# Tokens as the stationary side of the second MLP product in three of four groups, with the sums turned back by DVE and DMA

## The chip, the cores and the metric

One Trainium2 chip; the kernel runs on one of its cores. The metric is the time of one execution on the device in microseconds (us). The kernel before takes 1535.57 us, the median of 3 runs (1535.53 to 1535.76).

The engines are named as in the profile: PE is TensorE (matmul), PEld its loading of the stationary operand, DVE is VectorE, ACT ScalarE, POOL GpSimd, SP SyncE. In a matmul one operand stands still in the array (stationary, 128x128) and the other streams through (moving, up to 512 columns); the product has the stationary side's columns as its partitions and the moving side's columns as its row. Sums gather in PSUM, in banks of 512 columns.

## The reference

A decoder layer on 256 tokens (and 16 meta tokens) of width 2048: a token mixer, then a squared-ReLU MLP with 8192 inner columns, then a norm. The change touches the MLP alone:

```
def squared_relu_mlp(xn, w1, w2):
    return jnp.square(jax.nn.relu(xn @ w1)) @ w2
...
h = h + squared_relu_mlp(rmsnorm(h, norm_mlp_g[l]), w_ff1[l], w_ff2[l])
return rmsnorm(h, final_norm_g)[:, N_META:]
```

All in float32.

## The kernel before

**Layout.** The residual stream lies transposed in SBUF: `ht` is 128 partitions x 16 tiles x 256 tokens, where tile j holds model columns 128j to 128j+127 on the partitions. All operands are split in two parts for the multiplication, `hi` (rounded to the matmul's type) and `lo` (the rest), and a product is hi·hi + hi·lo + lo·hi.

**The MLP** runs over NG = 4 groups of 2048 inner columns (second half of `trunk`, the loop over `g`). In each group:

- *first product*, 16 steps f: `gemm2(next_weights(), x2)` makes one tile of 128 inner columns x 256 tokens; `relu2` squares it and splits it into `a[:, f, 0, :]` (hi) and `a[:, f, 1, :]` (lo);
- *second product*, 16 steps j: `gemm2(next_weights(), a)` makes one tile of 128 model columns x 256 tokens out of the group's 2048 inner columns, and `add_residual` adds it to `ht[:, j, :]`: one ACT copy of the second half of the bank and two DVE adds.

In the last group the last NL = 4 tiles are made apart, in two token halves, so that the final norm and the stores can start early; this part stays as it is.

**One `gemm2`** goes over k = 0 to 15 with two matmuls each (`mac2`). In both, the weights are the stationary side and tokens move: the weights' hi against 512 columns (the tokens' hi and lo, 256 each), and the weights' lo against 256 (the tokens' hi).

```
nc.tensor.matmul(steps(ps), hi, steps(row(x)), start=first, stop=False)
nc.tensor.matmul(steps(ps[:, 0:NT]), lo, steps(x[:, 0, :]), start=False, stop=last)
```

`steps` is an access that reads and writes the columns in runs of four elements, 16 apart, in four passes.

**The weights** lie in HBM as 128x2048 chunks in the order of use, `w_all`; a chunk of the second product has 16 k x 128 output columns. `next_weights` brings one in as two pieces (`weight_half`): SP issues one DMA of 512 KB (128 partitions x 4 KB) into a `raw` buffer, ACT casts it to `hi` (L126), DVE subtracts to `lo` (L127). There are five `raw` buffers and five of `w` (hi and lo). A `raw` buffer is free after DVE's subtraction, a `w` buffer after PE's last matmul on it.

**The order** on each engine is made by a scheduler ahead of time from the order of the code and a timeline of its own; each engine then works through its queue strictly in that order. Thus ACT's casts stand some pieces ahead of the copies that wait for PE. `later(n, fn)` holds a function back until n further products have been issued.

**Pools.** PSUM has the pools `pg` (3 banks) and `px` (5). In SBUF, `gat` holds the MLP's small tiles; its tag `o` (8 KB a partition, 2 buffers) serves the output at the end. `keep` with tag `s1` holds `a`.

Of the kernel before, what the change touches and what calls it, by code (L numbers as in the profile page):

```python
# [7 lines left out]
F32 = mybir.dt.float32  # L8
# [3 lines left out]
AF = mybir.ActivationFunctionType  # L12
ALU = mybir.AluOpType
# [3 lines left out]
P = 128  # L17
D = 2048
KT = D // P
# [9 lines left out]
NG = 4  # L29
MASKED = -1e30  # L30
BIG = 3.0e38
RAW = 5
NL = 4
# [32 lines left out]
def trunk(ctx: ExitStack, tc: tile.TileContext, hT, w_small, w_all, consts, w_alpha2, out):  # L66
    nc = tc.nc
    serial = [0]

    def nm(s):  # L70
        serial[0] += 1
        return f"{s}_{serial[0]}"

    const = ctx.enter_context(tc.tile_pool(name="const", bufs=1))
    keep = ctx.enter_context(tc.tile_pool(name="keep", bufs=1))
    wp = ctx.enter_context(tc.tile_pool(name="wp", bufs=5))
# [3 lines left out]
    px = ctx.enter_context(tc.tile_pool(name="px", bufs=5, space=PSUM))  # L80
# [3 lines left out]
    def bank(pool, s):  # L84
        return pool.tile([P, 512], F32, tag="bank", name=nm(s))
# [4 lines left out]
    def later(n, fn):  # L90
        waiting.append([n, fn])

    def issued():
        for e in list(waiting):
            e[0] -= 1
            if e[0] <= 0:
                waiting.remove(e)
                e[1]()
# [6 lines left out]
    chunk = [0]  # L105
    HK = KT // 2

    def pair(meta=False):
        n = HK * P
        w = wp.tile([P, 2 * n + 64], F32R, tag="w", name=nm("w"))  # L110
        a, b = (0, 20) if meta else (24, 24)
        return [w[:, at : at + n].rearrange("p (k m) -> p k m", m=P) for at in (a, n + b)]
# [18 lines left out]
    def next_weights(keep_hi=None, meta=False):  # L131
        c = chunk[0]
        chunk[0] += 1
        parts = []
        for i in range(2):
            hi, lo, step = weight_half(c, i, None if keep_hi is None else keep_hi[:, HK * i : HK * (i + 1), :], meta)
            step(0, HK)
            parts.append((hi, lo))
        return lambda k: (parts[k // HK][0][:, k % HK, :], parts[k // HK][1][:, k % HK, :])

    def steps(ap):

        return ap.rearrange("p (i a e) -> p a i e", a=4, e=4)
# [93 lines left out]
    def operand(pool, name, nk=KT, at=0, **kw):  # L237

        t = pool.tile([P, at + nk * 2 * NT], F32R, name=nm(name), **kw)
        return t[:, at:].rearrange("p (k o t) -> p k o t", o=2, t=NT)  # L240
# [18 lines left out]
    def take(*shape):  # L259
        n = 1  # L260
        for d in shape:
            n *= d
        ap = room[:, at_room[0] : at_room[0] + n]
        at_room[0] += n
        if len(shape) == 2:
            ap = ap.rearrange("p (a b) -> p a b", b=shape[1])
        return ap
# [4 lines left out]
    def gain(i, k):  # L272
        return h[:, k, NA + i : NA + i + 1]
# [8 lines left out]
    acc = take(4, NA)  # L282
# [50 lines left out]
    for s in range(KT // 2):  # L333
        if s + 3 < KT // 2:
            with tc.issue_after(load_stage(s + 3, 0).ins):
                load_h(nc.sync, 2 * s + 6, 2)
            last = load_stage(s + 3, 1).ins
        wa, wb = stages[s]
        for kk in range(2):
            k = 2 * s + kk  # L340
# [15 lines left out]
        at = [(w[0][:, c], w[1][:, c]) for w, n in ((wa, 4), (wb, 3)) for c in range(n)]  # L356
# [35 lines left out]
    for i in range(2):  # L392
        w = pair(meta=True)[0]
# [17 lines left out]
    both = take(NA)  # L411
# [252 lines left out]
    ps = bank(pg, "psa")  # L664
    for k in range(KT):
        if k == HK:
            norm1()
        w = small[k // HK][:, k % HK, :]
# [171 lines left out]
    for j0 in range(0, KT, 2):  # L840
        gates = ahead if j0 == 0 else [gate() for _ in range(4)]
        w = next_weights()
        for j in range(2):
            t = total(gemm2(w, of, k0=8 * j, nk=8))
            nc.vector.tensor_tensor(gates[2 * j], gates[2 * j], t, op=ALU.mult)
        for j in range(2):
            t = total(gemm2(next_weights(), og))
# [7 lines left out]
    gat = ctx.enter_context(tc.tile_pool(name="gat", bufs=2, reuse_waits="tile"))  # L855
# [3 lines left out]
    ht = h[:, :, NM:NA]  # L859
    x2 = operand(keep, "x2", at=56, tag="s2")  # L860

    def square_sum(j, acc):
        if j == 0:
            nc.scalar.activation(acc, ht[:, j, :], AF.Square)
        else:
            sq = gat.tile([P, NT], F32, tag="hsq", name=nm("hsq"))
            nc.scalar.activation(sq, ht[:, j, :], AF.Square)  # L867
            nc.gpsimd.tensor_tensor(acc, acc, sq, op=ALU.add)  # L868
# [22 lines left out]
    def relu2(a, f, ps):  # L891
# [3 lines left out]
        nc.vector.tensor_tensor(s, t, t, op=ALU.mult)  # L895
        split_to(a[:, f, 0, :], a[:, f, 1, :], s)

    acc = gat.tile([P, NT], F32, tag="acc", name="acc3", bufs=1)
    for g in range(NG):
        a = operand(keep, "a", at=16, tag="s1")  # L900
        held = []
        for f in range(KT):
            ps = gemm2(next_weights(), x2, pool=px if g == 0 and f < 3 else pg)
            if g == 0 and f == 0:
                held.append(ps)
                continue
            if g == 0 and f == 1:
                relu2(a, 0, held.pop())
            relu2(a, f, ps)
        last = g == NG - 1  # L910
        for j in range(KT - NL if last else KT):
            add_residual(j, gemm2(next_weights(), a))
            if last:
                square_sum(j, acc)
                nc.scalar.activation(ht[:, j, :], ht[:, j, :], AF.Identity, scale=gain(2, j))
                if j == 0:
                    tc.keep_in_program_order(nc.scalar.preload_act_table_set("natural_log_exp_and_others"))


    whi = keep.tile([P, 8 + NL * KT * P + 56], F32R, tag="s2", name="whi_last")[:, 8 : 8 + NL * KT * P].rearrange(  # L920
# [2 lines left out]
    for n in range(NL):  # L923
        j, ps = KT - NL + n, bank(pg if n < 3 else px, "ps")
        w = next_weights(whi[:, n])
# [148 lines left out]
```

## Time and profile before

| what | value |
|---|---|
| median of 3 runs | 1535.57 us (1535.53 to 1535.76) |
| the profiled execution, its own time | 1535.16 us |
| its span, first to last instruction | 1533.5 us |
| mean granted clock of TensorE | 0.998 |
| second product of the first group | from 925.17 us of the span |
| second product of the third group | from 1266.50 to 1351.84 us |
| `hi` cast on ACT (L126), 128x1024 | 1048 ns |
| `lo` subtraction on DVE (L127), 128x1024 | 1225 ns |
| DMA of one weight piece, issue to landing | 4.5 us median |

Times in the views count from the first instruction. A row of the timeline gives the start, the length, the engine, the line, output<-inputs and how many instructions were merged; a PE length is modelled and overlaps the next, so the distance between two starts is what a matmul costs. A row of the windows gives the length of the window, then busy us and number of instructions of PE, PEld, DVE, ACT and POOL, then the granted clock, the DMA engines' busy share and GB/s. A row of a group gives busy us and mean ns, then the idle time ahead and who ended it.

### The profile page before, as it was taken

What the parts mean: (1) busy time and instruction counts of PE and PEld (TensorE: products, weight loads), DVE (VectorE), ACT (ScalarE), POOL (GpSimd) and SP (SyncE); (2) the same over time, 40 slices, a digit from 0 to 9 for tenths busy, and PEclk for the clock granted to TensorE, in tenths of its full rate; (3) what the DMA queues carried; (4) which work ended last, traced back from release to release, by engine and by line L of the source; (5) the groups of instructions that cost most, each with busy time, mean ns of one, the idle gap of its engine ahead of it and who ended that gap; (6) DMA issues with size and microseconds to landing.
All of it is one profiled execution on the core that took longest, in us unless ns stands there. A gap on an engine that the chain in (4) does not pass through costs nothing.

```text
span 1533.5 us, 25353 instructions
## 1 busy us (share of the span) xinstructions
PE 1522.3 (99%) x9812; PEld 1399.9 (91%) x9812; DVE 1072.2 (70%) x1659; ACT 794.4 (52%) x1271; POOL 130.2 (8%) x213
## 2 busy tenths in 40 slices
PE   9999999999999999999999999999999999999997
PEld 8999999999999999999999999999999999999997
DVE  7898858586666666666787876667766776667665
ACT  7766444555555544544666544445444454444563
POOL 6012010111100000000011000000000000000012
PEclk9999999999999999999999999999999999999999
DMA  9545555565555565655565566655565556555562
GB/s 320 172 153 176 182 162 188 160 212 170 166 167 188 197 198 197 195 199 199 188 209 195 197 198 197 200 195 195 195 203 197 198 196 199 197 197 200 194 195 96
DMA packets 86600, 293.08 MB, mean 191 GB/s; under 512 B 9112, under 2 KB 16800, under 8 KB 86352
## 3 DMA queue, kind: packets, MB, share of 16 engines
q1 hardware_dynamic: 85872, 289.62, 57.4%
q8 instruction: 77, 1.26, 0.3%
q0 software_dynamic: 176, 1.12, 0.2%
q10 hardware_dynamic: 432, 0.72, 0.1%
q14 instruction: 43, 0.35, 0.1%
HBM read 289.32 MB, written 2.11 MB: 190 GB/s over the span
## 4 chain that ended last, share of the span: by engine, by line
PE 96%; DVE 2%; ACT 1%; issue 1%; DMA 0%; POOL 0%; SPq 0%; POOLq 0%; DVEq 0%; ACTq 0%
PE ps L149 50%; PE ps L150 26%; PE psa L154 5%; PE psa L158 4%; PE psa L156 4%; PE ps L364 1%; PE ps L943 1%; PE ps L366 1%; DVE w L127 1%; PE ps L927 0%; DMA raw<-w_all_dram 0%; PE pa L562 0%; PE po L620 0%; DVE room L434 0%; POOL o L991 0%
## 5 line engine op out<-in xcount | busy, mean ns | idle before, releaser
L127 DVE TENSOR_TENSOR w<-raw,w 128x1024 fp32r<-128x1024 f32 x522 | 644.8, 1235 | 260.5 <-ACT w L126 251.3
L126 ACT CAST w<-raw 128x1024 fp32r<-128x1024 f32 x522 | 547.1, 1048 | 275.2 <-PE ps L150 210.1
L149 PE MATMUL ps<-x,w 128*128 128x512 f32 x1952 | 654.7, 381 | 0.0
L150 PE MATMUL ps<-x,w 128*128 128x256 f32 x1952 | 535.7, 274 | 0.0
L149 PEld LDWEIGHTS ps<-x,w 128*128 128x128 f32 x1952 | 366.5, 188 | 62.4
L150 PEld LDWEIGHTS ps<-x,w 128*128 128x128 f32 x1952 | 366.7, 188 | 0.0
L149 PE MATMUL ps<-a,w 128*128 128x512 f32 x960 | 320.2, 380 | 0.0
L150 PE MATMUL ps<-a,w 128*128 128x256 f32 x960 | 263.3, 274 | 0.0
L149 PEld LDWEIGHTS ps<-a,w 128*128 128x128 f32 x960 | 180.3, 188 | 30.9
L154 PE MATMUL psa<-x,w 128*128 128x272 f32 x640 | 181.9, 285 | 0.0
L150 PEld LDWEIGHTS ps<-a,w 128*128 128x128 f32 x960 | 180.3, 188 | 0.0
L158 PE MATMUL psa<-x,w 128*128 128x272 f32 x640 | 179.8, 282 | 0.0
L156 PE MATMUL psa<-x,w 128*128 128x272 f32 x624 | 176.1, 282 | 0.0
L187 ACT COPY evb<-ps 128x256 f32<-128x256 f32 x160 | 59.4, 371 | 205.1 <-PE ps L150 203.5
L190 DVE TENSOR_TENSOR evt<-ps,evb 128x256 f32<-128x256 f32 x158 | 67.0, 424 | 80.1 <-ACT evb L187 79.7
L154 PEld LDWEIGHTS psa<-x,w 128*128 128x128 f32 x640 | 120.2, 188 | 0.2
L158 PEld LDWEIGHTS psa<-x,w 128*128 128x128 f32 x640 | 120.2, 188 | 0.1
L156 PEld LDWEIGHTS psa<-x,w 128*128 128x128 f32 x624 | 117.6, 188 | 0.0
L868 POOL TENSOR_TENSOR acc<-acc,hsq 128x256 f32<-128x256 f32 x26 | 26.5, 1017 | 737.6 <-ACT hsq L867 737.6
L149 PE MATMUL ps<-og,w 128*128 128x512 f32 x256 | 85.8, 380 | 0.0
L149 PE MATMUL ps<-y,w 128*128 128x512 f32 x256 | 85.4, 380 | 0.0
L872 ACT COPY evb<-ps 128x256 f32<-128x256 f32 x76 | 28.2, 371 | 103.3 <-PE ps L150 102.3
(297 smaller groups left out, 1471.2 us busy)
## 6 DMA issues: line engine op xcount, KB each, us to landing
raw<-w_all_dram SPq DMA_DIRECT2D x537, 512.0 KB, 4.5
raw<-w_all_dram SPq DMA_DIRECT2D x8, 384.0 KB, 6.7
h<-hT_dram SPq DMA_DIRECT2D x8, 275.0 KB, 6.8
negc<-fdram POOLq DMA_DIRECT2D x1, 1088.0 KB, 7.9
out_dram<-o SPq DMA_DIRECT2D x2, 512.0 KB, 2.6
raw<-w_all_dram SPq DMA_DIRECT2D x2, 256.0 KB, 3.7
room<-w_small_dram SPq DMA_DIRECT2D x1, 320.0 KB, 8.1
out_dram<-o ACTq DMA_DIRECT2D x1, 320.0 KB, 3.1
```

The source lines that it names most:

```text
L126: nc.scalar.copy(hi[:, k, :], r)
L127: nc.vector.tensor_tensor(lo[:, k, :], r, hi[:, k, :].bitcast(F32), op=ALU.subtract)
L149: nc.tensor.matmul(steps(ps), hi, steps(row(x)), start=first, stop=False)
L150: nc.tensor.matmul(steps(ps[:, 0:NT]), lo, steps(x[:, 0, :]), start=False, stop=last)
L154: nc.tensor.matmul(steps(ps[:, X_LO]), hi, steps(x_lo[:, k]), start=first, stop=False, skip_group_check=True)
L156: nc.tensor.matmul(steps(ps[:, 0:NA]), lo, steps(x_hi[:, k]), start=False, stop=last and hi is None, skip_group_check=True)
L158: nc.tensor.matmul(steps(ps[:, 0:NA]), hi, steps(x_hi[:, k]), start=False, stop=last, skip_group_check=True)
L187: nc.scalar.copy(b, ps[:, NT:512])
L190: nc.vector.tensor_tensor(t, ps[:, 0:NT], b, op=ALU.add)
L364: nc.tensor.matmul(steps(ps), hi, steps(row(x[:, k])), start=st, stop=False)
L868: nc.gpsimd.tensor_tensor(acc, acc, sq, op=ALU.add)
L872: nc.scalar.copy(b, ps[:, NT:512])
```

## The change

In groups 0 to 2 the second product has its sides exchanged. Its 2048 output columns are taken in four blocks b of 512. For each k, 128 tokens of `a` are the stationary side and 512 weight columns the moving one; two token halves t give two banks, `pt`. The six matmuls of a k are, for each t: a-hi with w-hi, a-hi with w-lo, a-lo with w-hi. The result has tokens on the partitions. It is gathered over the groups in a new tile `rows` (2 halves x 2048 columns; 16 KB a partition): copied by ACT in group 0, added by DVE in 1 and 2.

The weights of a block come from four chunks at once (`wide_weights`): each of its eight pieces has two k and four chunks' 128 columns, 512 KB as before in runs of 1 KB, and ACT and DVE write hi and lo so that the 512 columns of a k lie in a row.

In group 2, `turn_back(b)` brings a block back to the layout of `ht`: two DVE transposes of 32x32 squares, 16 DMAs from POOL's queue that move the squares between partition groups within one tile of tag `o` (32 partitions x 8 runs x 32 elements each, 32 KB), and four adds on POOL into `ht`. The last group's second product is as before.

```
+    def wide_weights(q):
+
+        c0, k0 = chunk[0], 4 * q
+        parts = []
+        for i in range(2):
+            raw = wp.tile([P, HK * P], F32, tag="raw", name=nm("raw"), bufs=RAW)
+            hi, lo = (t.rearrange("p k m -> p (k m)").rearrange("p (k c m) -> p k c m", k=2, m=P) for t in pair())
+            r = raw.rearrange("p (c k m) -> p c k m", k=2, m=P)
+            cols = slice((k0 + 2 * i) * P, (k0 + 2 * i + 2) * P)
+            nc.sync.dma_start(r, w_all[c0 : c0 + 4, :, cols].rearrange("c p (k m) -> p c k m", m=P))
+            r = r.rearrange("p c k m -> p k c m")
+            nc.scalar.copy(hi, r)
+            nc.vector.tensor_tensor(lo, r, hi.bitcast(F32), op=ALU.subtract)
+            parts.append([t.rearrange("p k c m -> p k (c m)") for t in (hi, lo)])
+        if q == 3:
+            chunk[0] += 4
+        return lambda k: tuple(t[:, k % 2, :] for t in parts[k % 4 // 2])
...
+    rows = gat.tile([P, 2, D], F32, name="rows", bufs=1)
+
+    def turn_back(b):
+
+        both = gat.tile([P, KT * P], F32, tag="o", name=nm("turn"))
+        tr = both[:, 0:1024].rearrange("p (t f) -> p t f", t=2)
+        for t in range(2):
+            nc.vector.transpose(tr[:, t, :], rows[:, t, 512 * b : 512 * b + 512])
+        back = both[:, 1024:]
+        for c in range(4):
+            for i in range(4):
+                src = both[32 * c : 32 * c + 32, 0:1024].rearrange("p (e i r) -> p e i r", i=4, r=32)[:, :, i, :]
+                dst = back[32 * i : 32 * i + 32].rearrange("p (e c r) -> p e c r", c=4, r=32)[:, :, c, :]
+                nc.gpsimd.dma_start(dst, src)
+        for j in range(4):
+            r = ht[:, 4 * b + j, :].rearrange("p (t r) -> p t r", t=2)
+            nc.gpsimd.tensor_tensor(r, r, back.rearrange("p (t j r) -> p t j r", t=2, j=4)[:, :, j, :], op=ALU.add)
+
+    def token_rows(g, b, a):
+
+        pt = [bank(px, "pt") for _ in range(2)]
+        for k in range(KT):
+            if k % 4 == 0:
+                w = wide_weights(k // 4)
+            hi, lo = w(k)
+            for t, ps in enumerate(pt):
+                ah, al = (a[:, k, o, P * t : P * t + P] for o in range(2))
+                nc.tensor.matmul(steps(ps), ah, steps(hi), start=(k == 0), stop=False)
+                nc.tensor.matmul(steps(ps), ah, steps(lo), start=False, stop=False)
+                nc.tensor.matmul(steps(ps), al, steps(hi), start=False, stop=(k == KT - 1))
+        issued()
+        for t, ps in enumerate(pt):
+            r = rows[:, t, 512 * b : 512 * b + 512]
+            if g == 0:
+                nc.scalar.copy(r, ps)
+            else:
+                nc.vector.tensor_tensor(r, ps, r, op=ALU.add)
+        if g == NG - 2:
+            later(2, lambda: turn_back(b))
+
     acc = gat.tile([P, NT], F32, tag="acc", name="acc3", bufs=1)
     for g in range(NG):
-        a = operand(keep, "a", at=16, tag="s1")
+        last = g == NG - 1
+        a = operand(keep, "a", at=16 if last else 48, tag="s1")
...
-        last = g == NG - 1
-        for j in range(KT - NL if last else KT):
+        if not last:
+            for b in range(4):
+                token_rows(g, b, a)
+            continue
+        for j in range(KT - NL):
             add_residual(j, gemm2(next_weights(), a))
-            if last:
-                square_sum(j, acc)
-                nc.scalar.activation(ht[:, j, :], ht[:, j, :], AF.Identity, scale=gain(2, j))
-                if j == 0:
-                    tc.keep_in_program_order(nc.scalar.preload_act_table_set("natural_log_exp_and_others"))
+            square_sum(j, acc)
+            nc.scalar.activation(ht[:, j, :], ht[:, j, :], AF.Identity, scale=gain(2, j))
+            if j == 0:
+                tc.keep_in_program_order(nc.scalar.preload_act_table_set("natural_log_exp_and_others"))
```

**DVE's queue in a second product.** Before, in the middle of one: the two adds of a tile j into `h`, the subtractions of two weight pieces, and again (a name with `raw` is the piece that came by DMA, `w` its hi and lo, `ps` the bank, `evb` ACT's copy).

```order
L873 TENSOR_TENSOR h_80<-ps_1477_10251,h_80 128x256
L874 TENSOR_TENSOR h_80<-h_80,evb_1478_10284 128x256
L127 TENSOR_TENSOR w_1492_10383<-raw_1491_10382,w_1492_10383 128x1024
L127 TENSOR_TENSOR w_1494_10388<-raw_1493_10387,w_1494_10388 128x1024
L873 TENSOR_TENSOR h_80<-ps_1483_10298,h_80 128x256
L874 TENSOR_TENSOR h_80<-h_80,evb_1484_10331 128x256
```

Of the change, at the end of the third group's second product: the two transposes of block 2 (right behind its adds into `rows`), the last four pieces of block 3 (L153), the first four of the last group (L127), then the adds and transposes of block 3. The first of the two transposes of `turn_1946` waits for the DMAs and for POOL's adds that use the buffer of `turn_1930`, block 1's; that of `turn_1937` likewise for `turn_1911`, block 0's.

```order
L923 STREAM_TRANSPOSE turn_1937_13537<-rows_9246 128x512 x2
L153 TENSOR_TENSOR w_1923_13401<-raw_1922_13400,w_1923_13401 128x1024
L153 TENSOR_TENSOR w_1925_13406<-raw_1924_13405,w_1925_13406 128x1024
L153 TENSOR_TENSOR w_1927_13435<-raw_1926_13434,w_1927_13435 128x1024
L153 TENSOR_TENSOR w_1929_13440<-raw_1928_13439,w_1929_13440 128x1024
L127 TENSOR_TENSOR w_1933_13495<-raw_1932_13494,w_1933_13495 128x1024
L127 TENSOR_TENSOR w_1935_13500<-raw_1934_13499,w_1935_13500 128x1024
L127 TENSOR_TENSOR w_1942_13570<-raw_1941_13569,w_1942_13570 128x1024
L127 TENSOR_TENSOR w_1944_13575<-raw_1943_13574,w_1944_13575 128x1024
L952 TENSOR_TENSOR rows_9246<-pt_1912_13330,rows_9246 128x512
L952 TENSOR_TENSOR rows_9246<-pt_1913_13331,rows_9246 128x512
L923 STREAM_TRANSPOSE turn_1946_13612<-rows_9246 128x512 x2
```

The adds into `h` after each tile are gone; a block's adds now come once in eight pieces, and the transposes stand right behind them, ahead of the next pieces. `later(2, ...)` has not moved them further back.

**POOL's queue in the MLP.** Before, nothing of POOL's stands between the last sum of squares ahead of the MLP (`acc2`) and the first of the last group (`acc3`).

```order
L868 TENSOR_TENSOR acc2_8414<-acc2_8414,hsq_1308_9138 128x256
L868 TENSOR_TENSOR acc2_8414<-acc2_8414,hsq_1315_9190 128x256
L868 TENSOR_TENSOR acc2_8414<-acc2_8414,hsq_1322_9242 128x256
L868 TENSOR_TENSOR acc3_9246<-acc3_9246,hsq_2142_14952 128x256
L868 TENSOR_TENSOR acc3_9246<-acc3_9246,hsq_2149_15003 128x256
```

Of the change, between the two: for each of the four blocks 16 DMAs and, when all of them have landed, four adds.

```order
L929 DMA turn_1911_13305<-turn_1911_13305 32x8x32 x16
L932 TENSOR_TENSOR h_80<-h_80,turn_1911_13305 128x256 x4
L929 DMA turn_1930_13468<-turn_1930_13468 32x8x32 x16
L932 TENSOR_TENSOR h_80<-h_80,turn_1930_13468 128x256 x4
L929 DMA turn_1937_13537<-turn_1937_13537 32x8x32 x16
L932 TENSOR_TENSOR h_80<-h_80,turn_1937_13537 128x256 x4
L929 DMA turn_1946_13612<-turn_1946_13612 32x8x32 x16
L932 TENSOR_TENSOR h_80<-h_80,turn_1946_13612 128x256 x4
L886 TENSOR_TENSOR acc3_9247<-acc3_9247,hsq_2074_14469 128x256
```

The first DMA of a block waits for the transposes; of its 16 DMAs the ninth waits for a signal that one of the first eight has landed, and so on, so that up to eight are under way.

## Prediction

> **What bounds the kernel now.** I read the page first: engine shares and the chain of waits.
>
> ```profile
> span 1533.5 us, 25353 instructions
> PE 1522.3 (99%) x9812; PEld 1399.9 (91%) x9812; DVE 1072.2 (70%) x1659; ACT 794.4 (52%) x1271; POOL 130.2 (8%) x213
> PE 96%; DVE 2%; ACT 1%; issue 1%; DMA 0%; POOL 0%; SPq 0%; POOLq 0%; DVEq 0%; ACTq 0%
> ```
>
> TensorE is the chain, and every matmul has its own weight load (9812 of each). A busy PE is not a PE at its peak, so the next view is the timeline of PE around the second product of the first MLP group, for the distance from start to start, and then the last rows before the end, where only 256-column matmuls run.
>
> ```profile
> 925.06 0.27 PE L150 MATMUL ps<-x,w 128*128 128x256 f32 x1
> 925.17 0.38 PE L149 MATMUL ps<-a,w 128*128 128x512 f32 x1
> 925.39 0.27 PE L150 MATMUL ps<-a,w 128*128 128x256 f32 x1
> ...
> 1010.39 0.28 PE L150 MATMUL ps<-a,w 128*128 128x256 f32 x1
> 1010.50 0.38 PE L149 MATMUL ps<-x,w 128*128 128x512 f32 x1
> ...
> 1511.79 3.45 PE L943 MATMUL ps<-a,whi_last 128*128 128x256 f32 x29
> ```
>
> The second product of a group starts at 925.17 and the next group at 1010.50: 85.33 us for 16 x 16 = 256 pairs, 333.3 ns a pair. The 29 matmuls of 256 columns take 28 steps plus one length of 0.28: (3.45 - 0.28) / 28 = 113.3 ns a step. So a 512-column one has 333.3 - 113.3 = 220.0 ns, as the starts 925.17 and 925.39 say. The difference of 106.7 ns for 256 columns is 0.4167 ns a column, which leaves 113.3 - 106.7 = **6.67 ns that every matmul pays, however wide**. There is nothing else to win on PE: 85.33 is 256 equal pairs, without a stall.
>
> Does anything else stand close to PE? The windows of the same 85 us and its groups:
>
> ```profile
> 0.00:50.00 50.00, 47.95 (x290) 42.45 (x291) 36.84 (x57) 34.20 (x54) 24.02 (x49) 1.00 0.89 287
> 925.00:1010.00 85.00, 85.00 (x511) 76.79 (x511) 53.14 (x68) 38.27 (x49) 0.00 (x0) 1.00 0.60 197
> L127 DVE TENSOR_TENSOR w<-raw,w 128x1024 fp32r<-128x1024 f32 x32 | 39.2, 1225 | 20.3 <-ACT w L126 19.4
> L126 ACT CAST w<-raw 128x1024 fp32r<-128x1024 f32 x32 | 33.5, 1048 | 23.1 <-PE ps L150 19.4 <-issue 3.7
> L873 DVE TENSOR_TENSOR h<-ps,h 128x256 f32<-128x256 f32 x15 | 6.4, 424 | 10.6 <-ACT evb L872 10.6
> ```
>
> PE 85 of 85 us, DVE 53, ACT 38, POOL 0, DMA 0.60, clock 1.00. The cast of a weight piece waits for PE to give a buffer back (19.4 us), so weights are always ahead: five buffers, one in use, four ready.
>
> **The change part by part.** *PE.* Per k and four output columns, before: 4 x (512 + 256) columns in 8 matmuls, 4 x 333.3 = 1333.3 ns. After: 2 token halves x 3 matmuls of 512, 6 x 220.0 = 1320.0. The columns are equal (3072 each); two matmuls fewer, 13.3 ns. Times 16 k, 4 blocks, 3 groups = 192: **-2.56 us**. A block then takes 16 x 1.32 = 21.1 us, a second product 84.5.
>
> The 220.0 was measured with x or a moving. After, the weight tiles move, which ACT and DVE are filling beside. Bounds for one matmul: below, the fixed 6.67 ns gone altogether, 1152 x 6.67 = -7.7 us more; above, the nearest row with other moving tiles, in plain order:
>
> ```profile
> 97.68 0.28 PE L620 MATMUL po<-a0l,v0h 128*128 128x256 f32 x1
> ...
> 98.74 0.28 PE L620 MATMUL po<-a0h,v0l 128*128 128x256 f32 x1
> ```
>
> Nine steps of 256 columns in 1.06 us are 117.8 ns, 4.5 above 113.3: 1152 x 4.5 = +5.2 us, twice that if it goes with the columns. I take 220.0, because the access in fours of elements is kept for the moving side, and x, a, and the others give the same 220 with it.
>
> The Trainium skill (TensorE: Matmul & The Clock Gate, "Wait — 56ns, not 53.3ns?") puts the fixed part of a warm matmul at about 2.5 ns, 215.7 ns for 512 columns. The trace disagrees for these matmuls: 220.0.
>
> *Weight pieces.* As many as before, 512 KB each, one per 2.64 us instead of 2.67, but in runs of 1 KB from four chunks. That form is in the trace, in the first 50 us (L292):
>
> ```profile
> L292 SPq DMA_DIRECT2D raw<-w_all_dram x17: 367/368/918, 1.2 to 26.0; - x17
> DMA to landing us min/median/max: 3.4/6.6/8.4
> ...
> raw<-w_all_dram SPq DMA_DIRECT2D x537, 512.0 KB, 4.5
> ```
>
> 0.37 us on SP; landing 6.6 us (at worst 8.4) at a DMA share of 0.89, against 4.5. A raw buffer's round is 0.37 + landing + cast 1.05 + subtraction 1.23, and five of them must not exceed 5 x 2.64 = 13.2: a landing of up to 10.5 us costs nothing, so both 4.5 and 8.4 give 0. In the first 50 us 287 GB/s came through; 199 are needed. ACT and DVE write the pieces with k and column exchanged, in runs of 128: the subtraction in the form of two such runs is the short one of this row, 433 ns for 256 elements against 424 for a plain one (L873 above). Cost 0 behind PE.
>
> ```profile
> L298 DVE TENSOR_TENSOR w<-raw,w x19: 433/954/1239, 5.3 to 34.7; 128x1024 fp32r<-128x1024 f32 x7, 128x768 fp32r<-128x768 f32 x7, 128x256 fp32r<-128x256 f32 x2, 128x384 fp32r<-128x384 f32 x2
> L298 DVE TENSOR_TENSOR w<-raw,w 128x512 fp32r<-128x512 f32 x1 | 0.7, 693 | 0.3 <-ACT w L297 0.3
> ```
>
> *Evacuation.* Per block, four ACT copies and eight DVE adds go; two adds of 128x512 (0.69 us each by the row above; copies on ACT in group 0) come. DVE gets 8 x 0.42 - 1.4 = 2.0 us freer per block, worth nothing beside a busy PE.
>
> *Turning back*, in the third group alone: per block two DVE transposes (no row; 0.69 us each as the same size), then 16 DMAs and four adds on POOL. Here a wait is added: **DVE's transposes of block 2 and 3 reuse the buffers of block 0 and 1**, so DVE stands still until POOL has done with those, and behind the transposes queue the subtractions that PE needs next. How long is a block on POOL?
>
> ```profile
> L464 POOL DMA_DIRECT2D fdram<-room x1: 705/705/705, 70.8 to 70.8; - x1
> L701 POOL DMA_DIRECT2D negc<-fdram x1: 598/598/598, 303.3 to 303.3; - x1
> DMA to landing us min/median/max: 3.3/5.6/7.9
> L868 POOL TENSOR_TENSOR acc<-acc,hsq x26: 735/892/1462, 769.6 to 1506.6; 128x256 f32<-128x256 f32 x26
> ```
>
> Low: 16 x 0.60 + 3.3 + 4 x 0.74 = 15.8 us. High, with twice the issue time since each DMA has 256 runs, the long landing and the slow adds: 16 x 1.41 + 7.9 + 4 x 1.46 = 36.3; farther out, each DMA landing before the next, 16 x 3.3 + 4 = 57, against which speaks that eight may be under way. I take X = 16 x 0.9 + 3.3 + 4 x 0.9 = 21 us, nearer the low end, because the two issues differ little whatever they carry.
>
> The dates, from the start of that product: block 0 ends at 21.1, DMAs from 23.9 (two adds, two transposes); block 1 is done on POOL at 23.9 + 2X; DVE comes to the transposes of block 3 at 84.5 + 1.4 = 85.9. DVE waits 2X - 62 us. Four pieces ahead cover 4 x 2.67 = 10.7 us of PE, less 2.8 for adds and transposes and 1.23 for the next subtraction: 6.6. So PE loses **2X - 68.6 us, nothing up to X = 34.3**. At 21: 0, with 20 us on DVE to spare. POOL's last block is done by about 85.9 + 1.4 + 21 = 108; the first sum that reads it, ht in the last group, comes after 16 first products, at 84.5 + 85.3 = 170. These DMAs bring 2 MB in all, on top of a DMA share of 0.60.
>
> The Trainium skill (DMA: Bandwidth & Descriptors, "Anatomy of one DMA — SWDGE (gpsimd) path") gives about 2.0 us fixed per such DMA. Taken one after another, as an estimate from that page, X would be 16 x 2.08 + 4 = 37 and PE would lose 6 us; the page also calls most of it completion, which overlaps. No row here shows sixteen in a row.
>
> **Sum.** PE -2.56, all else 0 behind PE. The profiled execution took 1535.16 us (span 1533.5 and 1.7 around it): 1532.6. The median shown is 1535.57, 0.4 above it: **1533.0 us**, 0.17% less.
>
> **Rivals.**
>
> 1. *POOL is slower than the transposes allow* (slower). Place: DVE at the third group's last transposes; deciding point X = 34.3. X = 45 costs 21 us: 1554; X = 53 costs 37: 1570. For it: nothing in the trace has 256 short runs in one DMA. Against: issues of 0.6 to 0.7 us. Chance 0.13.
> 2. *Moving weights is dearer* (slower): the 4.5 or 9 ns of above, 1538 to 1543; break-even is 2.2 ns. Against: the steady 220 with every tile so far. 0.13.
> 3. *Wide loads come late*: a landing of 11.5 us makes a piece 14.15 / 5 = 2.83 us, 0.19 x 96 = 18 us: 1551. Against: 8.4 at worst at 0.89. 0.06.
> 4. *The fixed part shrinks when the two sides change places* (faster): gone by half, 1152 x 3.3 = 3.8 us more, 1529; all of it, 1525. By the page's 2.5 ns it would be 1528. Against: it is the same 6.67 ns in all rows of this kind. 0.14.
> 5. *The change does not do what it says*: the two matmuls saved are given back at the twelve block ends or around the turn, 1 to 3 us: 1534 to 1536. Against: no stall at the block ends now, and four pieces stand ahead there. 0.10.
>
> My forecast has 0.44, its own range being 1532.3 to 1534.0.
>
> **How the numbers follow.** What a measurement here can tell from no change is about 0.2%, 3.07 us: below 1532.5 is faster, above 1538.6 slower. Faster: rival 4 and a small part of the forecast (0.08), 0.22. Same: the rest of the forecast 0.36, 0.07 of rival 5, 0.01 of rival 2, 0.44. Slower: 0.12 of rival 2, rivals 1 and 3, and 0.03 of rival 5, 0.34. The range 1529 to 1553 leaves out the far half of rival 4 (0.06) and the far ends of rivals 1 and 3 (0.08).
>
> **What would show it.** Steps of the 512-column matmuls with w moving: 220 ns right, above 222 rival 2, below 219 rival 4. A second product of 84.5 us in each of three groups. On POOL, first DMA of a block to its last add: about 21 us, and no wait of DVE's transposes for POOL; a PE gap some 10 us into the last group would be rival 1. Casts waiting for DMA instead of PE in the three products would be rival 3. I am wrong in kind if PE has any gap between 925 and 1432, wrong in size if the step is not 220.

## The result, and the profile after

| | before | change |
|---|---|---|
| median, 13 runs each | 1535.53 us (1534.37 to 1535.94) | 1538.28 us (1537.69 to 1540.38) |
| profiled execution, span | 1533.5 us | 1536.9 us |
| mean granted clock of TensorE | 0.998 | 0.999 |

The ratio is 1.002, with a 95% interval of 1.0011 to 1.0028: the change costs 2.75 us (0.18%) where 2.56 us less were forecast. So the question is where 5.3 us went. The page of the change, engine shares and chain:

```profile
span 1536.9 us, 24555 instructions
PE 1526.5 (99%) x9428; PEld 1386.3 (90%) x9428; DVE 1049.4 (68%) x1587; ACT 785.4 (51%) x1231; POOL 182.9 (12%) x293
PE 96%; DVE 2%; ACT 1%; issue 1%; POOL 0%; DMA 0%; POOLq 0%; DVEq 0%; ACTq 0%
```

PE issues 9812 - 9428 = 384 matmuls fewer, as the change says (2 x 192), and is still the chain, without a new wait. It has fewer matmuls of the same total of columns, and takes 4.2 us longer over them. The timeline of PE in the change, at the places where one product ends and the next begins (L167 and L168 are the former L149 and L150; L943 to L945 are the token rows):

```profile
925.04 0.38 PE L943 MATMUL pt<-w,a 128*128 128x512 f32 x1
...
1009.08 0.38 PE L944 MATMUL pt<-w,a 128*128 128x512 f32 x1
1009.30 0.40 PE L945 MATMUL pt<-w,a 128*128 128x512 f32 x1
1009.53 0.39 PE L167 MATMUL ps<-x,w 128*128 128x512 f32 x1
...
1096.58 0.38 PE L943 MATMUL pt<-w,a 128*128 128x512 f32 x1
...
1182.33 0.38 PE L167 MATMUL ps<-x,w 128*128 128x512 f32 x1
...
1267.68 0.38 PE L943 MATMUL pt<-w,a 128*128 128x512 f32 x1
...
1352.17 0.39 PE L167 MATMUL ps<-x,w 128*128 128x512 f32 x1
...
1439.21 0.39 PE L167 MATMUL ps<-a,w 128*128 128x512 f32 x1
...
1510.22 1.76 PE L1004 MATMUL ps<-a,whi_last 128*128 128x256 f32 x14
```

The differences of these starts are the lengths of the products. In the kernel before each had 85.33 us, and the last stretch 69.58 (from 1437.17 to 1506.75):

| product | second g0 | first g1 | second g1 | first g2 | second g2 | first g3 | last stretch |
|---|---|---|---|---|---|---|---|
| change | 84.49 | 87.05 | 85.75 | 85.35 | 84.49 | 87.04 | 71.01 |
| less before | -0.84 | **+1.72** | **+0.42** | +0.02 | -0.84 | **+1.71** | **+1.43** |

They sum to +3.6, against +3.4 in the span. Two of the three changed products came out at 84.49 as forecast. Most of the loss lies in products that **the change does not touch**, the first products of groups 1 and 3. Is it a stall or a slower step? The windows of the change, 80 us out of each of the six products in order, show it in the count behind PE's busy time:

```profile
928.00:1008.00 80.00, 80.00 (x366) 68.27 (x365) 37.30 (x32) 35.68 (x38) 0.00 (x0) 1.00 0.62 198
1012.00:1092.00 80.00, 80.00 (x472) 71.07 (x471) 57.60 (x87) 39.11 (x59) 0.00 (x0) 1.00 0.59 194
1100.00:1180.00 80.00, 80.00 (x360) 67.13 (x359) 40.70 (x37) 31.28 (x32) 0.00 (x0) 1.00 0.61 197
1185.00:1265.00 80.00, 80.00 (x482) 72.26 (x481) 58.74 (x88) 39.72 (x59) 0.00 (x0) 1.00 0.60 199
1270.00:1350.00 80.00, 80.00 (x366) 68.26 (x365) 45.70 (x45) 31.96 (x32) 35.96 (x57) 1.00 0.78 218
1356.00:1436.00 80.00, 80.00 (x472) 71.11 (x471) 59.56 (x88) 39.01 (x59) 12.51 (x19) 1.00 0.64 201
```

482 matmuls in the third group's first product (fourth row), 472 in the second's and fourth's; 366 token rows in groups 0 and 2, 360 in group 1. The clock is 1.00 throughout, PE has no gap, and the DMA share does not go with it (0.59, 0.61 and 0.64 in the long products, 0.60 to 0.78 in the quick ones). So the matmuls there are a little longer. The lengths give it exactly: 87.04 us / 256 = 340.0 ns a pair instead of 333.3, 85.75 us / 384 = 223.3 ns a token-row matmul instead of 220.0. Two matmuls of a pair share 6.7 ns, one token-row matmul has 3.3. Counted in columns of 0.4167 ns, a matmul has on the mean 24 of them on top of its own instead of 16: **10.0 ns instead of 6.67, on the mean**. It is not one fixed amount on each instruction. By the starts of single matmuls in the window from 1356 to 1436, one of 512 columns takes 225.4 ns and one of 256 takes 114.6, against 220.0 and 113.3 in the kernel before; the token rows of group 1 alternate between 222 and 225. PE has two rhythms, called quick (16) and long (24) from here on, and holds either for 85 us and more.

The change of rhythm comes where the operands exchange roles: quick to long at 1009.53, back at 1182.33, to long again at 1352.17. All three are ways back from token rows to weights as the stationary side; at the ways into token rows (925.04, 1096.58, 1267.68) the rhythm stays as it was. The rows around 1009 show the seam: the last token-row matmul takes 1009.53 - 1009.30 = 0.23 us, against 0.22 for the one before it.

What the change added elsewhere went as costed. POOL's timeline in the change (idle before and its releaser in brackets), its sources, and the groups and DMA issues that go with them:

```profile
1291.36 7.54 POOL L929 DMA_DIRECT2D turn<-turn  x13 [448.50 <-DVE turn L923]
1300.51 1.73 POOL L929 DMA_DIRECT2D turn<-turn  x3 [1.61 <-DMA turn<-turn]
1305.89 4.57 POOL L932 TENSOR_TENSOR h<-h,turn 128x256 f32<-128x256 f32 x4 [3.65 <-DMA turn<-turn]
...
1369.06 3.98 POOL L932 TENSOR_TENSOR h<-h,turn 128x256 f32<-128x256 f32 x4 [2.96 <-DMA turn<-turn]
```

```profile
L923 DVE STREAM_TRANSPOSE turn<-rows x8: 662/684/703, 1289.8 to 1354.1; 128x512 f32<-128x512 f32 x8
L929 POOL DMA_DIRECT2D turn<-turn x64: 582/582/651, 1291.4 to 1365.5; - x64
```

```profile
L152 ACT CAST w<-raw 128x1024 fp32r<-128x1024 f32 x96 | 100.4, 1046 | 129.9 <-PE pt L945 122.1
turn<-turn POOLq DMA_DIRECT2D x64, 32.0 KB, 4.5
```

Block 0 is on POOL from 1291.36 to 1305.89 + 4.57 = 1310.46, 19.1 us; the last add ends at 1373.04. The casts of the wide pieces wait for PE, 122.1 us of 129.9, and none for a DMA.

### The profile page after: what moved, and what is told of

It reads as the page before. It is cut to its first block, busy times and chain, and to the rows that moved or that the text cites. A ratio compares the mean times of both kernels' runs of the same rounds, so it can differ in the third digit from the quotient of the medians.

```text
span 1536.9 us, 24555 instructions
## 1 busy us (share of the span) xinstructions
PE 1526.5 (99%) x9428; PEld 1386.3 (90%) x9428; DVE 1049.4 (68%) x1587; ACT 785.4 (51%) x1231; POOL 182.9 (12%) x293
## 4 chain that ended last, share of the span: by engine, by line
PE 96%; DVE 2%; ACT 1%; issue 1%; POOL 0%; DMA 0%; POOLq 0%; DVEq 0%; ACTq 0%
PE ps L167 40%; PE ps L168 20%; PE pt L944 6%; PE pt L943 6%; PE pt L945 6%; PE psa L172 5%; PE psa L176 4%; PE psa L174 4%; PE ps L382 1%; PE ps L384 1%; PE ps L1004 1%; DVE w L127 1%; PE ps L988 0%; PE pa L580 0%; PE po L638 0%
## 5 line engine op out<-in xcount | busy, mean ns | idle before, releaser
L127 DVE TENSOR_TENSOR w<-raw,w 128x1024 fp32r<-128x1024 f32 x426 | 528.2, 1240 | 215.5 <-ACT w L126 209.6
L167 PE MATMUL ps<-x,w 128*128 128x512 f32 x1952 | 658.1, 383 | 0.0
L126 ACT CAST w<-raw 128x1024 fp32r<-128x1024 f32 x426 | 446.7, 1049 | 223.3 <-PE ps L168 146.5
L168 PE MATMUL ps<-x,w 128*128 128x256 f32 x1952 | 536.3, 275 | 0.0
L167 PEld LDWEIGHTS ps<-x,w 128*128 128x128 f32 x1952 | 366.3, 188 | 65.4
L168 PEld LDWEIGHTS ps<-x,w 128*128 128x128 f32 x1952 | 366.4, 188 | 0.2
L153 DVE TENSOR_TENSOR w<-raw,w 128x1024 fp32r<-128x1024 f32 x96 | 118.4, 1233 | 106.6 <-ACT w L152 106.1
L152 ACT CAST w<-raw 128x1024 fp32r<-128x1024 f32 x96 | 100.4, 1046 | 129.9 <-PE pt L945 122.1
L205 ACT COPY evb<-ps 128x256 f32<-128x256 f32 x160 | 59.5, 372 | 206.7 <-PE ps L168 205.0
L945 PE MATMUL pt<-w,a 128*128 128x512 f32 x384 | 146.5, 381 | 0.0
L944 PE MATMUL pt<-w,a 128*128 128x512 f32 x384 | 146.4, 381 | 0.0
L943 PE MATMUL pt<-w,a 128*128 128x512 f32 x384 | 146.4, 381 | 0.0
L929 POOL DMA_DIRECT2D turn<-turn x64 | 36.9, 584 | 462.4 <-DVE turn L923 457.3
L167 PE MATMUL ps<-og,w 128*128 128x512 f32 x256 | 85.8, 380 | 0.0
L167 PE MATMUL ps<-y,w 128*128 128x512 f32 x256 | 85.4, 380 | 0.0
```

What stands on the lines that cost most here:

```text
L126: nc.scalar.copy(hi[:, k, :], r)
L127: nc.vector.tensor_tensor(lo[:, k, :], r, hi[:, k, :].bitcast(F32), op=ALU.subtract)
L152: nc.scalar.copy(hi, r)
L153: nc.vector.tensor_tensor(lo, r, hi.bitcast(F32), op=ALU.subtract)
L943: nc.tensor.matmul(steps(ps), ah, steps(hi), start=(k == 0), stop=False)
L944: nc.tensor.matmul(steps(ps), ah, steps(lo), start=False, stop=False)
```

## The experiments

Each time is that of one profiled execution, unless said otherwise. The kernel before, measured together with them, took 1535.26 us beside e1 to e4, 1535.84 beside f1 to f5, 1534.85 beside g1, g2, h1 and the timed e3, and 1535.15 beside h2 and h3. Lengths of products are differences of starts in the timeline, as above.

### Is it the turning back? How many seams?

**e1**: the change without `turn_back`; the sums of the first three groups are never added to `ht`.

```
-        if g == NG - 2:
-            later(2, lambda: turn_back(b))
```

> Left out: the turning back, so the second products of the first three groups are never added to the residual stream. Theory A (PE keeps one of two steady rhythms, 6.67 or 10.0 ns a matmul above its columns, and the way back from token rows to weights as the stationary side flips it): the last group stays slow, first product 87.0 us, and the time stays within 0.7 us of the change. Theory B (the turning back, its 64 DMAs and DVE's transposes, slows PE or its supply): the 3 us or so lost in the last group come back, time 1535.0 to 1535.5, first product of the last group 85.3.

1538.15 us, the change's time. The lengths are the change's too: 84.49, 87.05, 85.75, 85.35, 84.49, 87.04, and 70.72 for the last stretch. The window of the fourth group's first product in e1, with nothing on POOL and no transposes:

```profile
1356.00:1436.00 80.00, 80.00 (x473) 71.09 (x472) 58.46 (x88) 38.80 (x58) 0.00 (x0) 1.00 0.58 195
```

The same long rhythm at a DMA share of 0.58: the 64 DMAs, POOL's adds and the transposes cost the path at most the 0.3 us of the last stretch.

**e2**: token rows in the third group alone (`a` at 48 there, at 16 elsewhere).

```
-            if g == 0:
+            if g == NG - 2:
...
+        if g < NG - 2:
+            for j in range(KT):
+                add_residual(j, gemm2(next_weights(), a))
+            continue
```

> Token rows in the third group alone, the first two as in the kernel before. Theory A: one flip, at the end of the third group. The first two groups at 85.33 us a product, the third's second product 84.49, the last group slow: first product 87.04, the rest 1.4 us longer; time 2.3 us above the kernel before. Theory B: the same last group only if the turning back is what slows it. Theory C (each changed group costs its own share, about 0.9 us): 0.9 us above.

1536.90 us, +1.64 where theory A had 2.3. All five products ahead have 85.33, the token rows 84.49, what follows 87.04 and 70.72. Windows of e2, the second group's first product and the fourth's:

```profile
1012.00:1092.00 80.00, 80.00 (x482) 72.25 (x481) 58.84 (x89) 39.77 (x59) 0.00 (x0) 1.00 0.59 198
1356.00:1436.00 80.00, 80.00 (x472) 71.08 (x471) 59.58 (x88) 39.72 (x59) 9.99 (x15) 1.00 0.61 200
```

One way back, one switch to the long rhythm: -0.84 + 1.71 + 1.14 = +2.0 in the products.

### A neutral matmul at the seam

**e3**: the change with one matmul of 256 columns (`kick` in the code and the views) between the last token rows and the next first product, into a bank that nobody reads. It moves its columns in plain order, not through `steps`; its bank comes from `px`, while the first products of groups 1 to 3 use `pg`, so it shifts no bank of the product behind it.

```
+    def kick(lhs, rhs):
+        ps = bank(px, "kick")
+        nc.tensor.matmul(ps[:, 0 : rhs.shape[-1]], lhs, rhs, start=True, stop=True)
...
+            kick(ones_r[:, 0:P], x2[:, 0, 0, :])
```

> The change, with one matmul more (ones as the stationary side, 256 columns of x2 moving, into a bank that nobody reads) at each of the three ways back from token rows to weights as the stationary side; its own cost 3 x 0.113 us. Theory A: what happens at the way back sets the rhythm, so products that were slow (87.05, 85.74, 87.04 us) come out at 85.33, 84.49, 85.33, or others become slow; the lengths jump between these pairs of values and take none between. Theory B or C: all lengths as in the change, time 0.3 us above it.

1532.88 us. Every product is quick: 84.48 for the three with token rows, 85.35 for the first ones, 69.58 at the end. Theory A held here, the lengths jumped from the one value to the other. Three matmuls more make the change 5.4 us shorter.

**e4**: the kernel before with neutral matmuls at the ends of groups 0, 1 and 2 (256 columns, 64 columns, and 256 with `a` as stationary side).

```
+        if g == 0:
+            kick(ones_r[:, 0:P], x2[:, 0, 0, :])
+        elif g == 1:
+            kick(ones_r[:, 0:P], x2[:, 0, 0, 0:64])
+        elif g == 2:
+            kick(a[:, 0, 0, 0:P], x2[:, 0, 0, :])
```

> The kernel before, with one matmul more at the end of the first, second and third group (ones with 256 columns of x2; ones with 64 columns; a with 256 columns of x2). Theory A: a disturbance alone can flip the rhythm: products after one of them take 87.04 instead of 85.33 us, 1.7 us each until the next flip, the time up to 8 us above the kernel before. Theories B and C: every product 85.33 us, the time 0.3 us above.

1536.31 us, but not by a switch: the products stay at 85.33 to 85.46. The last stretch has 70.19 us, with a stall near its end (0.16 us of PE waiting for DVE there is the only wait that the trace names). Theory A had it that a disturbance alone can flip the rhythm; none of these three did. It took more to see when one does.

### Which property of the seam?

**f1**: e3 with the last weight piece as the neutral matmul's stationary side. **f2**: the change with the last two matmuls of a block exchanged, so that `lo` moves last. **f5**: the kernel before with one matmul in which weights move (`a` stationary, 512 columns of the last piece, through `steps`) at the end of group 0.

```
+            kick(hi[:, 0:P], x2[:, 0, 0, :])                    # f1
...
+                if k == KT - 1:                                  # f2
+                    last.reverse()
...
+        if g == 0:                                               # f5
+            kick(a[:, 0, 0, 0:P], w.flat)
```

> As the change with the neutral matmul at the three ways back, but its stationary side comes from the last weight piece (w) instead of from the ones; it still moves 256 columns of x2. Theory A1 (the rhythm flips where a stationary side is loaded from w while a w tile is moving): this load is then such a one, so the products are slow again as in the change, 87.05, 85.75, 87.04 us, time about 1538.4. Theory A0 (any matmul between the two forms keeps the rhythm): all products fast, 85.35 and 84.49, time about 1532.9.

> The change; at the last k alone the second and third matmul of a token half change places, so that the last to move is w-lo and not w-hi, at no cost. Theory A1 in its bare form: slow as the change, 1538.3. Theory A2 (it takes the same place within the two w tiles: hi moving while a hi is loaded, both 24 words into their buffers): fast, 1532.6 or so. If the rhythm has to do with neither, no difference.

> The kernel before, with one matmul more at the end of the first group: a as the stationary side and 512 columns of the last weight piece moving, into a bank that nobody reads; its own cost 0.22 us. Theory A1: the next load, from w, falls under a moving w, PE goes over to the slow rhythm, and with no second such place it stays there: five products 1.71 us longer each and the rest 1.1, some 9 to 10 us in all, 1545. Theory A0 or any that needs token rows themselves: 1535.6.

f1: 1533.14 us, all products quick; its last stretch has 70.07 us, with steps of 0.22 to 0.32 us among its 256-column matmuls. f2: 1538.47 us, lengths as in the change (87.05, 85.75, 87.04). f5: 1535.16 us, no switch, 85.33 to 85.35. So it is neither a load of the stationary side out of the buffers that just moved (f1), nor which of hi and lo comes last (f2), nor by itself that a weight tile moves just ahead of the seam (f5).

**f3**: `a` at 16 words into its buffer in all groups, as before the change, instead of 48. **h1**: at 80, 64 words away from 16.

```
-        a = operand(keep, "a", at=16 if last else 48, tag="s1")
+        a = operand(keep, "a", at=16, tag="s1")                  # h1: 80 for 16 where not last
```

> The change with a 16 words into its buffer in all groups, instead of 48 in the first three. Theories A1 and A2: a's place has no part in the way back, so slow products as in the change, 1538.3. If the place of the stationary side against the moving one decides (theory A3), the token rows themselves change their step away from 220.0 ns or the flips change.

> The change with a 80 words into its buffer in the first three groups. With 48 a step of the token rows took 220.0 ns (223.3 in the slow rhythm), with 16 226.7. If only the place within 64 words counts (80 is 16 + 64): 226.7 again, second products 87.03 and no slow first products, 1540.2. If within 32 words: all three of 16, 48 and 80 would have been alike, which 16 and 48 already exclude. If the distance from the start of the buffer itself counts: another step.

1540.19 and 1540.20 us. In both the token rows take 87.03 us, and all else is quick (85.35, 69.58). The window of the first token rows in f3, to be held against the 366 of the change:

```profile
928.00:1008.00 80.00, 80.00 (x355) 66.16 (x354) 36.18 (x32) 34.83 (x37) 0.00 (x0) 1.00 0.58 192
```

87.03 / 384 = 226.6 ns a matmul: on the mean 32 columns' time on top of the 512, 13.3 ns. The single steps repeat 229, 220, 224, 227, 233 ns. Where the stationary tiles lie sets the step of the token rows, alike for two places 64 words apart. And out of this third rhythm the way back always led to the quick one.

### Does the length decide?

**g1**: e3 with 264 columns instead of 256. **g2**: the kernel before with 264, 272 and 248 columns at the ends of groups 0, 1 and 2.

```
-            kick(ones_r[:, 0:P], x2[:, 0, 0, :])                 # g1, against e3
+            kick(ones_r[:, 0:P], row(x2[:, 0])[:, 0:264])
...
+        if not last:                                             # g2, against before
+            kick(ones_r[:, 0:P], row(x2[:, 0])[:, 0 : (264, 272, 248)[g]])
```

> The change with the neutral matmul at the three ways back, of 264 columns instead of 256 (3.3 ns longer). Theory A4 (the rhythm is a matter of when the next product starts: 264 is half of a 16-column step off): slow again, in all or some of the products that the change has slow, 1536 to 1539. Theory A0 (any matmul between the two forms lets PE settle into the quick rhythm): 85.35 and 84.49 throughout, 1532.9.

> The kernel before with a neutral matmul at the end of the first three groups, of 264, 272 and 248 columns. Theory A4: the one of 264 throws PE into the slow rhythm, 87.04 us a product, until one of the next two brings it back: 2 to 10 us above the kernel before. Theory A0 (only the way back from token rows can leave PE in the slow rhythm): products of 85.33 to 85.5 us, 0.4 to 0.6 us above.

g1: 1532.76 us, all quick, as theory A0 had it and not A4. g2: 1538.79 us. PE's timeline in g2 at the two first kicks (the line above each is the last matmul of a second product):

```profile
1010.14 0.27 PE L150 MATMUL ps<-a,w 128*128 128x256 f32 x1
1010.26 0.28 PE L900 MATMUL kick<-x,ones 128*128 128x264 f32 x1
1010.38 0.39 PE L149 MATMUL ps<-x,w 128*128 128x512 f32 x1
...
1184.48 0.29 PE L900 MATMUL kick<-x,ones 128*128 128x272 f32 x1
1184.61 0.38 PE L149 MATMUL ps<-x,w 128*128 128x512 f32 x1
```

From 1010.38 to 1184.48 are 174.10 us for 512 pairs, 340.0 ns each: both products long, in the kernel before, with no token rows in it. A matmul of 0.12 us cost 3.4 us. After 272 columns the two products are quick again (85.35, 85.33), and the 248 columns changed nothing.

That is what theory A4 had forecast for g2, and A0 had not. So 264 columns switch the rhythm at this seam and not at the way back from token rows.

**h2** and **h3** make a table of it: a neutral matmul behind 93 tiles of the first three groups in the kernel before, 128 to 512 columns in steps of 8, shuffled, in two different orders.

```
+            if g < NG - 1 and (g or f >= 3):
+                kick(ones_r[:, 0:P], row(x2[:, 0])[:, 0 : next(lengths)])
...
+            if not last:
+                kick(ones_r[:, 0:P], row(x2[:, 0])[:, 0 : next(lengths)])
```

> The kernel before, with one neutral matmul (128 to 512 columns in steps of 8, in a shuffled order, into a bank that nobody reads) behind 93 of the 96 tiles of the first three MLP groups. A tile of 16 pairs takes 16 x 333.3 = 5.33 us in the quick rhythm and 16 x 340.0 = 5.44 in the long one, so each tile tells the rhythm that the neutral matmul ahead of it left. Theory L (the rhythm is a phase that the columns shift): whether a tile after it is quick or long follows from the number of columns and the rhythm ahead of it alone, lengths that are whole multiples of 16 leave the rhythm as it is, and those with 8 over change it, in most of about 47 such cases. Theory R (the flip of the earlier run was chance or a matter of the place): at most a few of the tiles are long, and no order by columns shows. Time: under R 1535 + 93 x 0.14 = 1548; under L up to 3 us more.

> The same with the lengths in another order, so that each length stands behind other tiles and other rhythms. Theory L: the same table of length and rhythm ahead against rhythm behind as in the run before it, with few exceptions. Theory R: other lengths flip than there.

1556.02 and 1552.82 us, above the 1548 to 1551 expected. The 93 neutral matmuls cost 13.8 us in each, the tiles of the first three groups 4.2 and 4.5 us more than in the kernel before; and in h2 the last neutral matmul (240 columns, long ahead of it) left the whole fourth group long, 87.04 and 70.72 us against 85.35 and 69.58 in h3. The first three kicks of h2 in PE's timeline:

```profile
861.22 0.23 PE L900 MATMUL kick<-x,ones 128*128 128x144 f32 x1
861.29 0.43 PE L149 MATMUL ps<-x,w 128*128 128x512 f32 x1
...
866.76 0.35 PE L900 MATMUL kick<-x,ones 128*128 128x416 f32 x1
866.95 0.38 PE L149 MATMUL ps<-x,w 128*128 128x512 f32 x1
...
872.30 0.39 PE L900 MATMUL kick<-x,ones 128*128 128x488 f32 x1
```

The tile after 144 columns has 866.76 - 861.29 = 5.47 us, the one after 416 has 872.30 - 866.95 = 5.35: long, then quick. The table goes by the last pairs of each tile, since some lengths disturb only the first ones: after 136 columns from the quick rhythm the first five pairs take 340 to 384 ns and the rest 333.3, and such a tile counts as quick. Over both kernels:

| rhythm ahead | trials | quick after | long after |
|---|---|---|---|
| quick | 150 | 122 | 28 |
| long | 36 | 27 | 9 |

From the quick rhythm **the number of columns decides alone**, at these seams between tiles of pairs: 144, 168, 176, 184, 192, 264, 296, 312 and 360 led to the long one, each of the 28 times that they came, and the 40 other lengths never did, in either order. No length gave two answers. It fits that 264 flipped in g2 and 248 did not, nor 256 in e4 or 512 in f5. From the long rhythm 27 of 36 led back; here 240 and 376 gave both answers, so length and rhythm ahead do not decide alone. So theory L held for the quick rhythm and not for the long one, and its guess at the rule (8 over a multiple of 16) did not hold: 144 flips, 136 does not.

### The version that beats both

**e3 again**, timed over 11 executions.

> The change with the neutral matmul of 256 columns at the three ways back, timed. Theory A: the forecast of 2.56 us less, less 0.4 us for the three matmuls, holds for every execution: 1533.0 to 1533.4 against 1535.5, ratio 0.9983 to 0.9986. If the slow rhythm still comes in some executions, their times spread upward by 1.3 to 1.7 us a product.

1532.90 us, median of 11 runs (1532.58 to 1534.49), against 1534.85 for the kernel before in 15 runs: ratio 0.9988, interval 0.9979 to 0.9997. That is 1.95 us less, where 2.56 less 0.4 for the three matmuls were expected; the expected ratio, 0.9983 to 0.9986, lies inside the interval. Windows of it, the first token rows, the second group's first product, the third group's token rows:

```profile
928.00:1008.00 80.00, 80.00 (x366) 68.28 (x365) 37.18 (x32) 35.58 (x38) 0.00 (x0) 1.00 0.59 198
1012.00:1092.00 80.00, 80.00 (x482) 72.23 (x481) 58.89 (x89) 39.76 (x59) 0.00 (x0) 1.00 0.58 197
1270.00:1350.00 80.00, 80.00 (x367) 68.33 (x366) 45.94 (x45) 31.99 (x31) 39.21 (x60) 1.00 0.75 217
```

## Why the prediction was wrong

**The step that failed** is "PE -2.56, all else 0 behind PE", with the sentence it rests on, that every matmul pays 6.67 ns, however wide. The 6.67 ns were taken for a property of the instruction. They are the mean of a rhythm that PE is in, and the change moves PE out of it at two of its three ways back, into one with 10.0 ns. Term by term, against the kernel before: the three changed products were to bring -2.56 and brought -0.84 + 0.42 - 0.84 = -1.26; the products that were costed at nothing because nothing in them changes brought +1.72 + 0.02 + 1.71 + 1.43 = +4.9.

**Right, at these sizes:**

- A second product of 84.5 us: 84.49 in groups 0 and 2, and 84.48 in all three once the rhythm is held (e3). The median of e3, 1532.90, is close to what the forecast had for the change (1533.0), but partly by luck: the kernel before, measured together with it, took 0.7 us less than the 1535.57 that the forecast started from.
- POOL: X was put at 21 us and is 19.1 for block 0, with the last add at 1373.04 - 1267.68 = 105 us after the product's start (108). The row of waits named for rival 1 is absent, and by e1 the whole of it costs 0.3 us at most. The limit of X = 34.3 was not tried.
- Wide pieces cost nothing: casts wait for PE in the three products, not for a DMA.
- Transposes of 684 ns (0.69), POOL issues of 582 ns (0.6 to 0.9).

By the estimate from the Trainium skill (DMA: Bandwidth & Descriptors, "Anatomy of one DMA — SWDGE (gpsimd) path") X would have been 37 us, had the sixteen DMAs been paid one after another. Here they overlap: block 0 has 14.5 us from the first issue to the first add, at a median of 4.5 us of landing for each.

**The rivals.** Rival 2 had moving weights dearer, break-even at 2.2 ns a matmul. Group 1's token rows are dearer by 3.3, which looks like it; but groups 0 and 2 have 220.0 with the same tiles moving, and the first products, where no weight moves, carry most of the loss. The time of rival 2 (1538 to 1543) holds the result by another mechanism. Rivals 1 and 3 did not occur. Rival 4 had the direction reversed: the fixed part does change with what is beside it, and it grew. Rival 5, the saving given back at the block ends or at the turn, named the right kind of place, the seam, but as a stall of 1 to 3 us there. The seam itself costs some 10 ns by the rows at 1009; the rest is paid over the one or two products behind it, 87 to 173 us.

**What the view of before could have shown.** The timeline of the kernel before, shortly ahead of the rows that gave 113.3 ns:

```profile
1501.17 5.74 PE L927 MATMUL ps<-a,w 128*128 128x256 f32 x48
1506.75 1.75 PE L943 MATMUL ps<-a,whi_last 128*128 128x256 f32 x14
```

(1.75 - 0.28) / 13 = 113.1 ns a step below, (5.74 - 0.28) / 47 = 116.2 above. A dearer price stood a few rows away from the one that was used, for the same shape and with nothing on PE's way, so "the same 6.67 ns in all rows of this kind" (rival 4) did not hold in the kernel before. The same 48 matmuls in e1, where the pairs ahead of them run in the long rhythm:

```profile
1504.30 5.60 PE L986 MATMUL ps<-a,w 128*128 128x256 f32 x48
```

(5.60 - 0.28) / 47 = 113.2 ns. By the starts of single matmuls, in every run here they keep to 113 or 114 ns each behind long pairs (e1, e2, f2, h2, and the change up to a stall in their last third), and go between 109 and 125, 116.3 on the mean, behind quick ones wherever no stall falls among them. So what is left behind at a seam is not simply a dear state: it is dear for the pairs and cheap for these. The 117.8 ns of L620 that bounded rival 2 may be the same thing; that was not tried.

**What stays open.** Why the direct way back from quick token rows leads into the long rhythm in each of the cases (two in the change, two in e1, two in f2, one in e2), while a matmul of 256 or 264 columns in between prevents it. Other lengths were not tried at that place. h2 and h3 show that from the quick rhythm such a switch is decided by the length at a seam and is repeatable, not why these lengths do it. That the place of `a` sets the step of the token rows would fit loads of the stationary side and reads of the moving side meeting in memory; this is an argument, and no run shows the two meeting.

## What to carry to other kernels

A fixed cost per instruction that is read off a steady stretch belongs to that stretch: ask whether the pattern around it holds after the edit, and look in the trace for the same shape at another price before multiplying it by a thousand. After an edit at a bound engine compare the step in **every** stage, the untouched ones first; here the windows' instruction counts (472 against 482 in 80 us) showed the loss in one column. Where an engine falls into a worse rhythm at a seam, one cheap instruction at that place can be worth many times its own time: 0.12 us three times over made 5.4 us.

## What the hardware showed that was not expected

- PE with its weight loads runs in lasting rhythms at full clock (1.00): on the mean 16, 24 or 32 columns' time on top of a matmul's own columns, that is 6.67, 10.0 or 13.3 ns. The first is even (220.0 and 113.3 ns); the others are repeating patterns (222 and 225 ns in the token rows of the change's group 1, 220 to 234 in f3). The longest stretch seen in the long one is 174 us (g2). The Trainium skill (TensorE: Matmul & The Clock Gate, "Wait — 56ns, not 53.3ns?") knows one fixed part, about 2.5 ns; no product of the MLP ran at it here, 6.67 ns is the least.
- One matmul of 0.12 us can switch it, and from the quick rhythm, between tiles of pairs, its number of columns alone tells whether it does (28 of 28 for nine lengths, 0 of 122 for the others).
- A stationary operand at 48 words in its buffer gave 220.0 ns a step (223.3 in the long rhythm), at 16 and at 80 words 226.6, all else equal.
- The rhythm ahead can be dear for one shape and cheap for the next: 48 matmuls of 256 columns took 113.3 ns each behind long pairs (e1, h2) and 116.3 behind quick ones (the kernel before, h3).
